# Gate and up blocks of a macaron layer: a second weight sum by accumulating DMA, the lower right tile's product moved to third place, one bank seeded by ScalarE

## The chip, the cores and the metric

The kernel runs on one core of one Trainium2 chip. The metric is the time of one execution on the device, in microseconds; lower is better. Runs of the kernel before: 1727.0, 1727.16 and 1728.76 us, median 1727.16 us.

## What is computed

One decoder layer on a 256 x 2048 float32 input: a half-step SwiGLU FFN, a token mixer with two head groups, a second half-step FFN, a last norm. The change sits in the FFNs:

```python
def swiglu_ffn(x, w_gate, w_up, w_down):
    return (jax.nn.silu(x @ w_gate) * (x @ w_up)) @ w_down

x = x + FFN_RESIDUAL_SCALE * swiglu_ffn(rms_norm(x, ffn1_norm[l]), ...)   # 2048 -> 5632 -> 2048
...
x = x + FFN_RESIDUAL_SCALE * swiglu_ffn(rms_norm(x, ffn2_norm[l]), ...)
return rms_norm(x, final_norm)
```

## The kernel before, in words

**Arithmetic.** Every float32 matrix product is made of three products of rounded parts: both operands are split into a high part (a cast to the float32r type) and a low part (the rest), and hi x hi, lo x hi and hi x lo are added up in PSUM. `parts_of` (L214) splits a weight tile of 128 x 2048 (512 rows of the matrix by 512 columns): two casts of 128 x 1024 on ScalarE make the high part, one subtraction on VectorE makes the low part. Splits go round three pairs of buffers (`split_tiles`, L198), so a cast waits until TensorE has done with the high part made three splits earlier.

**Gate and up blocks.** The 5632 columns of the hidden layer are walked in one first block of 512 columns and five steps s = 0 to 4 of 1024 columns; in each step one block for the gate matrix (`g`) and one for the up matrix (`u`). After s = 0, 2 and 4 a down projection follows (`down`, L793). A gate or up block is one call of `seven` (L417). It handles 2048 rows by 1024 columns of weights: the upper 1024 rows as a 2 x 2 arrangement of tiles w11, w12, w21, w22 by a scheme of seven products in place of eight (two token tiles, two row halves, two column halves), the lower 1024 rows by plain products.

- The seven products, each 12 matmuls of 512 columns (`product_of`, L448): p0 with w11, p4 with w11 + w12, p5 with w11 + w12 + w22, p6 with w12 + w22, p2 with w22, p3 with the sum of p5 plus w21, p1 with w21. The stationary operands (`sf`) are sums of activation tiles made earlier.
- Plain products, each 24 matmuls on two banks (`usual`, L451): b2 and b3 for the right column half, a2 and a3 for the left one.
- Weight sums: w11 += w12, w11 += w22, w11 += w21 on VectorE (L463, L486, L514), in place; w12 += w22 by an accumulating DMA that GpSimd issues (L464).
- PSUM: four banks a, c, e, d. `snap` (L443) copies a bank to SBUF on ScalarE: s1 = a after p0, s5 = c after p4, u2 = -a after p5, u3 = -a after p6. `done(t, n, bank, snapshots)` hands over an output tile: `gate` (L879) or `up` (L884) adds the snapshots to the bank on VectorE (`total`, L871), then SiLU on ScalarE or the product with the gate.
- Order on TensorE: p0, p4, b2, p5, b3, p6, p2, a2, p3, a3, p1. The output tiles are done in the order (1,1) after p6, (0,1) after p2, (1,0) after a3, (0,0) after p1, the last with s1.

**Loads.** All weights come by DMAs on SP's queue, 1 MB each, in the order of `get` (L432): w11, w12, b2, w22, b3, a2, w21, a3. w11 and w12 lie in a pool of two buffers (`kept`), the others in three (`raws`, L81). SP issues in order, and a load waits for its buffer's last reader.

**What sets the order.** The tile framework's planner orders each engine's instructions by data flow and its own estimates; `held` (L41) pins an engine to program order for a while. So a line's place in the program isn't its place on the engine: casts and sums of the next products are moved ahead. Blocks also contain the transposes of finished hidden tiles (`turn_hidden`, L536, called by `settle`).

Of the kernel before, what the change touches and what calls it, by code (L numbers as in the profile page):

```python
# [13 lines left out]
ALU = mybir.AluOpType  # L14
AX = mybir.AxisListType

P = 128
D = 2048
S = 256
FF = 5632  # L20
NT = S // P
# [4 lines left out]
UK = 4  # L26
NH = 8
EPS = 1e-6
SQRT_FLOOR = 2.0**-114


class Engine:
# [17 lines left out]
def hybrid_block(ctx: ExitStack, tc: tile.TileContext, a: dict, out: bass.AP):  # L50
    nc = tc.nc
    Engine.pinned = False
    dve, act, pe, sp = (Engine(tc, e) for e in (nc.vector, nc.scalar, nc.tensor, nc.sync))
# [30 lines left out]

    def bank(name):
        return psum.tile([P, 512], F32, tag="ps", name=name)

    def f32(ap):
        return ap.bitcast(F32)
# [9 lines left out]
    ident = const.tile([P, P], F32, name="ident")  # L99
# [3 lines left out]
    early = const.tile([P, 1], F32, name="early")  # L103
# [110 lines left out]
    def parts_of(raw, name):  # L214
        hi, lo = split_tiles(name)
        for h in (slice(0, 2), slice(2, UK)):
            act.copy(hi[:, h, :], raw[:, h, :])
        low_part(raw, hi, lo)
        return blocks(hi, lo)
# [194 lines left out]
    def quad(tile):  # L414
        return tile.rearrange("p (j c) -> p j c", j=UK)

    def seven(w, rows, cols, sf, xs, name, keep, done, between=None, early=False, own=None, factor=None):  # L417

        apart = {}
        if own:
            a, c = (bank(f"ps_{name}_{n}") for n in "ac")
            apart.update({(t, 1): bank(f"ps_{name}_x{t}1") for t in range(NT)})
            d, e = bank(f"ps_{name}_d"), None
            apart.update({(t, 0): bank(f"ps_{name}_x{t}0") for t in range(NT)})
        else:
            a, c, e, d = (bank(f"ps_{name}_{n}") for n in "aced")  # L430

        def get(u, n, kept=False):  # L432
            src = w[u * UK * P : (u + 1) * UK * P, cols[n] : cols[n] + CW]
            return load(src, f"{name}_{u}{n}", kept=kept)

        (r0, r1), two = rows, len(xs) > 1
        w11, w12 = get(r0, 0, True), get(r0, 1, True)
        b2, w22 = get(xs[0][0], 1), get(r1, 1)
        b3 = get(xs[1][0], 1) if two else None
        a2, w21 = get(xs[0][0], 0), get(r1, 0)  # L440
        a3 = get(xs[1][0], 0) if two else None

        def snap(ps, n, scale=1.0):  # L443
            s = keep(f"{n}_{name}")
            act.activation(s, ps, AF.Copy, scale=factor[n] if factor else scale)
            return s

        def product_of(i, raw, ps, begin=False, end=True, blk=None):  # L448
            multiply([(ps, sf[i], begin, end)], blk or parts_of(raw, f"{name}_p{i}"), True)

        def usual(i, raw, n, *targets, first=None):  # L451

            blk = first or parts_of(raw, f"{name}_x{i}{n}")
            if own:
                last = i == len(xs) - 1
                targets = [(apart[t, n], t, i == 0, last) for t in range(NT)]
            multiply([(ps, stationary(xs[i][1], t), b, z) for ps, t, b, z in targets], blk, True)
            if own and last:
                for t in range(NT):
                    own(t, n, apart[t, n])  # L460

        product_of(0, w11, a, True)
        dve.tensor_tensor(w11, w12, w11, op=ALU.add)  # L463
        nc.gpsimd.dma_start(w12, w22, accum_op=ALU.add)  # L464
        if early:
            between("first sum")
        product_of(4, w11, c, True)
        blk = None
        if early:
            between("second product")  # L470
            hi, lo = split_tiles(f"{name}_x01")
            act.copy(hi, b2)
            s1 = snap(a, "s1")
            dve.tensor_tensor(w11, w22, w11, op=ALU.add)
            low_part(b2, hi, lo)
            blk = blocks(hi, lo)
        else:
            s1 = snap(a, "s1")
        s5 = snap(c, "s5")
        if between:  # L480
            between(0)
        usual(0, b2, 1, (e, 1, True, not two), (c, 0, False, False), first=blk)
        if between:
            between(1)
        if not early:
            dve.tensor_tensor(w11, w22, w11, op=ALU.add)  # L486
        if between:
            between("sum")
        product_of(5, w11, a)
        blk = blk2 = None  # L490
        if early:
            blk = parts_of(b3, f"{name}_x11")
            hi2, lo2 = split_tiles(f"{name}_p2")
            act.copy(hi2, w22)
            blk2 = blocks(hi2, lo2)
        u2 = snap(a, "u2", -1.0)
        if between:
            between(2)
        if two:
            usual(1, b3, 1, (e, 1, False, True), (c, 0, False, False), first=blk)  # L500
        if early:
            between("third sum")
        if early:
            low_part(w22, hi2, lo2)
            between("third low")
        product_of(6, w12, a)
        u3 = snap(a, "u3", -1.0)
        if early:
            between("fifth product")
        done(1, 1, e, [u3, s5])  # L510
        product_of(2, w22, c, blk=blk2)
        done(0, 1, c, [u2])
        usual(0, a2, 0, (d, 0, True, False), (a, 1, False, False))
        dve.tensor_tensor(w11, w21, w11, op=ALU.add)  # L514
        product_of(3, w11, a, end=own is not None or not two)
        if early:
            between("sixth product")
        if two:
            usual(1, a3, 0, (a, 1, False, True), (d, 0, False, False))
        done(1, 0, a, [])  # L520
        product_of(1, w21, d, own is not None)
        done(0, 0, d, [s1])

    def ffn(tag, norm, after, opening=False):
        with tc.tile_pool(name=f"ffn{tag}", bufs=1, side="left") as fp:
            more_from(fp)
            wg, wu, wd = (a[f"ffn{tag}_w_{s}"][0] for s in ("gate", "up", "down"))
# [8 lines left out]
            def turn_hidden(u, t, h, again):  # L536

                if u not in hidden:
                    hidden[u] = big(f"h{tag}_{u}")
                pt = bank(f"ph{tag}_{u}_{t}")  # L540
                for j in range(UK):
                    pe.transpose(pt[:, j * P : (j + 1) * P], h[:, j * P : (j + 1) * P], ident)
                pt = pt.rearrange("p (j c) -> p j c", j=UK)
                hi = hidden[u][:, :, t * P : (t + 1) * P]
                lo = hidden[u][:, :, S + t * P : S + (t + 1) * P]
                act.copy(hi, pt)
                dve.tensor_tensor(lo, pt, f32(hi), op=ALU.subtract)
                if again:
                    act.copy(quad(h), pt)
                    turned[u, t] = quad(h)  # L550

            def settle():
                while waiting:
                    turn_hidden(*waiting.pop(0))
# [3 lines left out]
            units, vs, sf, xn = {}, {}, {}, {}  # L558
# [84 lines left out]
            ps = {(m, t): bank(f"ps_{m}{tag}_0_{t}") for m in "gu" for t in range(NT)}  # L643
# [223 lines left out]
            for s in range(5):  # L867
# [22 lines left out]
                def meanwhile(i):  # L890
# [19 lines left out]
                    elif s == 0 and i == 0:  # L910
                        sums()

                seven(wg, (0, 1), cs, sf, xs, f"g{tag}_{s}", keep, gate, meanwhile, opening and s == 0)
                sp.held = False
                seven(
                    wu, (0, 1), cs, sf, xs, f"u{tag}_{s}", keep, up,
                    (lambda i: settle() if i == 1 else None) if opening and s == 0 else None, 
                )
                if s % 2 == 0:
                    down(s == 4)  # L920
# [49 lines left out]
    with tc.tile_pool(name="mixer", bufs=1, side="left") as mp, tc.tile_pool(name="mixw", bufs=2, side="left") as mw:  # L970
# [171 lines left out]
        def sc_c(between):  # L1142
# [10 lines left out]
            def turn(n):  # L1153
                for f in range(0, 4, 2):
                    pt = bank(f"pt_c{n}_{f}")
                    for i in range(2):
                        for t in range(NT):
                            o = i * S + t * P
                            pe.transpose(pt[:, o : o + P], z[t, n][:, (f + i) * P : (f + i + 1) * P], ident)
                    for i in range(2):  # L1160
                        q = 4 * (1 - n) + f + i
                        c = tmp("cc", q, S + 2, bufs=8)
                        nc.gpsimd.memset(c[:, :2], 0.0)
                        act.copy(c[:, 2:], pt[:, i * S : (i + 1) * S])
                        cc[q] = c

            def done(t, n, ps, tiles):
                for p in tiles[1:]:
                    dve.tensor_tensor(tiles[0], tiles[0], p, op=ALU.add)
                    free.append(p)  # L1170
                if tiles:
                    z[t, n] = tiles[0]
                    dve.scalar_tensor_tensor(z[t, n], ps, rt[t], z[t, n], op0=ALU.mult, op1=ALU.add)
                else:
                    z[t, n] = free.pop()
                    act.activation(z[t, n], ps, AF.Copy, scale=rt[t])
                if (t, n) == (1, 0):
                    turn(1)
# [226 lines left out]
```

## Time and profile before

| | |
|---|---|
| median of 3 runs | 1727.16 us |
| the profiled execution | 1726.91 us |
| its span, first to last instruction | 1725.1 us |
| granted TensorE clock, mean | 0.999 |
| median landing of a 1 MB load of raw_d | 5.2 us |
| HBM read | 339.82 MB |

Each line of the profile names a line of the program, an engine and an operation; the recording helper of the kernel gives nearly all of them line 43, so groups are told apart by their tiles: `hi_u_p` and `lo_u_p` are the parts of an up block's operand of one of the seven products, `hi_u_x` of a plain one, `raw_u` a loaded weight tile, `ps_u_a` the bank a of an up block, `s_u` and `u_u` its snapshots; `g` in place of `u` for gate, `d` for down. A row of the timeline has the start, the time (from the first start to the last end of a merged run, in us), the engine, the operation, output<-input, shapes and the count; in brackets the engine's idle time ahead of it and what ended it. A row of a stretch has its bounds, its length, and for PE, PEld (weight loads), DVE, ACT and POOL the busy time and the count, then the granted clock, the DMA engines' share and GB/s. A row of the view of waits has the waiting instruction, what it waited for, total us, how often, and the longest.

### The profile page before, as it was taken

The page shows a single profiled execution, that of the slowest core. Times are in us where ns is not written, and L with a number is a line of the kernel's source. Part 1 is how long each engine was busy: PE and PEld are TensorE (multiplying, and loading weights), DVE is VectorE, ACT ScalarE, POOL GpSimd, SP SyncE. Part 2 cuts the span into 40 slices and gives each one's busy share as a digit, 9 for nine tenths or more (in the row PEclk, how much of TensorE's full clock was granted, in tenths as well). Part 3 has the DMA queues.
Part 4 walks back from the last instruction along what each step waited for, and adds up shares of the span by engine and source line. Part 5 has one row for each costly group of instructions (what it writes and reads, how often), then busy time and mean ns, then how long its engine had stood idle before and what let it go on. Part 6 is the DMA issues. An engine that isn't in the chain of part 4 may idle for free.

```text
span 1725.1 us, 20426 instructions
## 1 busy us (share of the span) xinstructions
PE 1715.3 (99%) x7985; PEld 1432.9 (83%) x7985; DVE 1452.2 (84%) x1212; ACT 1077.8 (62%) x1406; POOL 35.3 (2%) x62
## 2 busy tenths in 40 slices
PE   9999999999999999999999999999999999999998
PEld 8888888888888888888888888888888888888886
DVE  7988889789789888787897889889788887788886
ACT  7666566656466656666965657655556664556664
POOL 0010000000000000000000000000000000000000
PEclk9999999999999999999999999999999999999999
DMA  8775777667677766655556675776777757677753
GB/s 300 225 258 174 242 234 227 214 236 233 182 238 226 227 201 219 211 160 193 175 197 205 204 251 165 228 237 224 230 227 219 244 171 243 214 225 220 254 179 128
DMA packets 178256, 372.59 MB, mean 216 GB/s; under 512 B 6132, under 2 KB 9072, under 8 KB 174448
## 3 DMA queue, kind: packets, MB, share of 16 engines
q1 hardware_dynamic: 173632, 340.81, 58.4%
q0 software_dynamic: 4352, 29.43, 8.5%
q8 instruction: 62, 1.02, 0.2%
q10 hardware_dynamic: 176, 1.06, 0.2%
q14 instruction: 34, 0.28, 0.0%
HBM read 339.82 MB, written 2.10 MB: 198 GB/s over the span
## 4 chain that ended last, share of the span: by engine, by line
PE 99%; DVE 0%; ACT 0%; DVEq 0%; issue 0%; ACTq 0%
PE ps_d L43 14%; PE ps_in L43 10%; PE ps_g_a L43 9%; PE ps_u_a L43 9%; PE ps_g_c L43 6%; PE ps_u_c L43 6%; PE ps_d_a L43 5%; PE ps_u_d L43 5%; PE ps_g_d L43 5%; PE ps_d_c L43 3%; PE ps_u_e L43 3%; PE ps_g_e L43 3%; PE ps_g L43 3%; PE ps_o L43 3%; PE ps_u L43 3%; PE ps_d_d L43 3%
## 5 line engine op out<-in xcount | busy, mean ns | idle before, releaser
L43 ACT CAST hi_g_p<-raw_g 128x1024 fp32r<-128x1024 f32 (+1 forms) x139 | 142.1, 1054 | 111.6 <-DVE raw_g L43 26.9
L43 DVE TENSOR_TENSOR lo_g_p<-raw_g,hi_g_p 128x2048 fp32r<-128x2048 f32 x70 | 159.8, 2289 | 42.3 <-ACT hi_g_p L43 41.6
L43 DVE TENSOR_TENSOR lo_u_p<-raw_u,hi_u_p 128x2048 fp32r<-128x2048 f32 x70 | 159.3, 2288 | 39.5 <-ACT hi_u_p L43 39.2
L43 ACT CAST hi_u_p<-raw_u 128x1024 fp32r<-128x1024 f32 x140 | 141.3, 1047 | 70.1 <-issue 23.1
L43 PE MATMUL ps_d<-hi_d,h 128*128 128x512 f32 x696 | 166.0, 390 | 0.0
L43 PEld LDWEIGHTS ps_d<-hi_d,h 128*128 128x128 f32 x696 | 130.0, 188 | 26.6
L43 ACT CAST hi_d<-raw_d 128x1024 fp32r<-128x1024 f32 x88 | 88.6, 1048 | 68.3 <-PE ps_u_d L43 19.9
L43 DVE TENSOR_TENSOR lo_d<-raw_d,hi_d 128x2048 fp32r<-128x2048 f32 x44 | 100.8, 2290 | 29.3 <-ACT hi_d L43 29.3
L43 PE MATMUL ps_in<-xT_nm,hi_in 128*128 128x512 f32 x512 | 122.5, 391 | 0.0
L43 ACT CAST hi_d_p<-raw_d 128x1024 fp32r<-128x1024 f32 x84 | 85.2, 1048 | 59.2 <-DVE raw_d L43 33.7
L43 PEld LDWEIGHTS ps_in<-xT_nm,hi_in 128*128 128x128 f32 x512 | 94.0, 188 | 18.8 <-ACT tha L43 0.5
L43 DVE TENSOR_TENSOR lo_d_p<-raw_d,hi_d_p 128x2048 fp32r<-128x2048 f32 x42 | 95.5, 2288 | 15.5 <-ACT hi_d_p L43 15.4
L43 ACT CAST hi_g_x<-raw_g 128x1024 fp32r<-128x1024 f32 (+1 forms) x79 | 81.2, 1058 | 42.9 <-PE ps_g_c L43 25.6
L43 ACT CAST hi_u_x<-raw_u 128x1024 fp32r<-128x1024 f32 x80 | 80.5, 1046 | 36.4 <-PE ps_u_c L43 22.1
L43 DVE TENSOR_TENSOR lo_g_x<-raw_g,hi_g_x 128x2048 fp32r<-128x2048 f32 x40 | 91.5, 2288 | 9.2 <-ACT hi_g_x L43 8.9
L43 DVE TENSOR_TENSOR lo_in<-raw_in,hi_in 128x2048 fp32r<-128x2048 f32 x32 | 73.2, 2288 | 26.7 <-ACT hi_in L43 26.3
L43 DVE TENSOR_TENSOR lo_u_x<-raw_u,hi_u_x 128x2048 fp32r<-128x2048 f32 x40 | 91.4, 2286 | 1.4 <-ACT hi_u_x L43 0.8
L43 PE MATMUL ps_d<-lo_d,h 128*128 128x512 f32 x348 | 86.2, 389 | 0.0
L43 ACT CAST hi_in<-raw_in 128x1024 fp32r<-128x1024 f32 x64 | 64.0, 1045 | 24.9 <-PE ps_in L43 15.2
L43 PEld LDWEIGHTS ps_d<-lo_d,h 128*128 128x128 f32 x348 | 65.3, 188 | 13.6
L43 DVE TENSOR_TENSOR raw_u<-raw_u,raw_u 128x2048 f32<-128x2048 f32 x30 | 68.7, 2289 | 8.5 <-DMA raw_u<-in_ffn_w_up_dram 8.1
L43 DVE TENSOR_TENSOR raw_g<-raw_g,raw_g 128x2048 f32<-128x2048 f32 x30 | 68.7, 2289 | 5.7 <-DMA raw_g<-in_ffn_w_gate_dram 5.2
(477 smaller groups left out, 3750.5 us busy)
## 6 DMA issues: line engine op xcount, KB each, us to landing
raw_d<-in_ffn_w_down_dram SPq DMA_DIRECT2D x88, 1024.0 KB, 5.2
raw_u<-in_ffn_w_up_dram SPq DMA_DIRECT2D x87, 1024.0 KB, 5.3
raw_g<-in_ffn_w_gate_dram SPq DMA_DIRECT2D x86, 1024.0 KB, 5.2
raw_in<-in_w_in_dram SPq DMA_DIRECT2D x32, 1024.0 KB, 5.1
raw_g<-raw_g POOLq DMA_DIRECT2D x10, 1024.0 KB, 7.0
raw_u<-raw_u POOLq DMA_DIRECT2D x10, 1024.0 KB, 7.0
raw_in_c<-in_w_in_dram SPq DMA_DIRECT2D x8, 1024.0 KB, 5.3
raw_o<-in_w_out_dram SPq DMA_DIRECT2D x8, 1024.0 KB, 5.2
```

The source lines that it names most:

```text
L43: ins = getattr(self.engine, name)(*args, **kwargs)
```

## The change

In 16 calls of `seven` (gate and up, s = 1 to 4, both FFNs; `moved=s > 0`) another order is taken. s = 0, the down projections and the mixer stay on the old path.

- **Third weight sum.** p3's operand is finished by a second accumulating DMA, w11 += w21, issued by GpSimd behind p5's split. VectorE's sum is gone. w21 is loaded ahead of a2.
- **p2 third.** The product with w22 follows p4, into bank c on top of it; s5 must be taken out of c in between. The output tile (0,1) is then done after b3, before p6.
- **Seed.** In place of the snapshot s1, ScalarE copies bank a to bank d after p0, and a2 adds onto it without a start flag. The tile (0,0) needs no VectorE add. One block, `g1_3` (`PARTLY`), keeps the snapshot.
- u3 and the split of p3's operand are pinned on ScalarE to program order (`act.held`).
- Transposes in `turn_hidden` and in the mixer's `turn` go through a helper that sets the start flag on the first of four only.

```diff
-        a2, w21 = get(xs[0][0], 0), get(r1, 0)
+        if not moved:
+            a2, w21 = get(xs[0][0], 0), get(r1, 0)
+        else:
+            w21, a2 = get(r1, 0), get(xs[0][0], 0)
...
+        if moved:
+            first = parts_of(w11, f"{name}_p0")
+            dve.tensor_tensor(w11, w12, w11, op=ALU.add)
+            nc.gpsimd.dma_start(w12, w22, accum_op=ALU.add)
+            seeded = name not in PARTLY
+            product_of(0, None, a, True, blk=first)
+            if seeded:
+                act.copy(d, a)
+                s1 = []
+            else:
+                s1 = [snap(a, "s1")]
+            product_of(4, w11, c, True)
+            s5 = [snap(c, "s5")]
+            if between:
+                between(0)
+            product_of(2, w22, c)
+            usual(0, b2, 1, (e, 1, True, not two), (c, 0, False, False))
...
+            dve.tensor_tensor(w11, w22, w11, op=ALU.add)
...
+            product_of(5, w11, a)
+            nc.gpsimd.dma_start(w11, w21, accum_op=ALU.add)
+            u2 = snap(a, "u2", -1.0)
...
+            if two:
+                usual(1, b3, 1, (e, 1, False, True), (c, 0, False, True))
+            done(0, 1, c, [u2])
+            product_of(6, w12, a)
+            act.held = True
+            u3 = snap(a, "u3", -1.0)
+            act.held = False
+            done(1, 1, e, [u3] + s5)
+            usual(0, a2, 0, (d, 0, not seeded, False), (a, 1, False, False))
+            act.held = True
+            fourth = parts_of(w11, f"{name}_p3")
+            act.held = False
+            product_of(3, None, a, end=not two, blk=fourth)
+            if two:
+                usual(1, a3, 0, (a, 1, False, True), (d, 0, False, False))
+            done(1, 0, a, [])
+            product_of(1, w21, d)
+            done(0, 0, d, s1)
+            return
```

The helper for transposes, and one of its two places:

```diff
+    def turn_into(ps, sources):
+        for i, src in enumerate(sources):
+            pe.matmul(
+                ps[:, i * P : (i + 1) * P], src, ident, is_transpose=True, start=i == 0, stop=True,
+                skip_group_check=True,
+            )
...
-                for j in range(UK):
-                    pe.transpose(pt[:, j * P : (j + 1) * P], h[:, j * P : (j + 1) * P], ident)
+                turn_into(pt, [h[:, j * P : (j + 1) * P] for j in range(UK)])
```

More of the change, by code (lines that the diff above doesn't have):

```diff
@@ L29 @@
 SQRT_FLOOR = 2.0**-114
+PARTLY = ("g1_3",)
 class Engine:
@@ L415, in quad, with seven @@
         return tile.rearrange("p (j c) -> p j c", j=UK)
-    def seven(w, rows, cols, sf, xs, name, keep, done, between=None, early=False, own=None, factor=None):
+    def seven(w, rows, cols, sf, xs, name, keep, done, between=None, early=False, own=None, factor=None, moved=False):
         apart = {}
@@ L460, in usual @@
                     own(t, n, apart[t, n])
+        if moved:
[15 more added lines that the diff above has]
+            usual(0, b2, 1, (e, 1, True, not two), (c, 0, False, False))
+            if between:
+                between(1)
+            dve.tensor_tensor(w11, w22, w11, op=ALU.add)
+            if between:
+                between("sum")
+            product_of(5, w11, a)
+            nc.gpsimd.dma_start(w11, w21, accum_op=ALU.add)
+            u2 = snap(a, "u2", -1.0)
+            if between:
+                between(2)
+            if two:
[17 more added lines that the diff above has]
+            return
         product_of(0, w11, a, True)
@@ L911, in meanwhile @@
                         sums()
-                seven(wg, (0, 1), cs, sf, xs, f"g{tag}_{s}", keep, gate, meanwhile, opening and s == 0)
+                seven(
+                    wg, (0, 1), cs, sf, xs, f"g{tag}_{s}", keep, gate, meanwhile, opening and s == 0, moved=s > 0,
+                )
                 sp.held = False
@@ L916, in ffn @@
                     wu, (0, 1), cs, sf, xs, f"u{tag}_{s}", keep, up,
-                    (lambda i: settle() if i == 1 else None) if opening and s == 0 else None,
+                    (lambda i: settle() if i == 1 else None) if opening and s == 0 else None, moved=s > 0,
                 )
@@ L1155, in turn @@
                     pt = bank(f"pt_c{n}_{f}")
[L1156 to L1159, printed above, removed]
+                    turn_into(
+                        pt, [z[t, n][:, (f + i) * P : (f + i + 1) * P] for i in range(2) for t in range(NT)]
+                    )
                     for i in range(2):
```

## The prediction

> **What bounds the kernel now.** I read the page first, then the view of waits for TensorE alone, then busy time by stretches.
>
> ```profile
> span 1725.1 us, 20426 instructions
> PE 1715.3 (99%) x7985; PEld 1432.9 (83%) x7985; DVE 1452.2 (84%) x1212; ACT 1077.8 (62%) x1406; POOL 35.3 (2%) x62
> PEclk9999999999999999999999999999999999999999
> q1 hardware_dynamic: 173632, 340.81, 58.4%
> q0 software_dynamic: 4352, 29.43, 8.5%
> PE 99%; DVE 0%; ACT 0%; DVEq 0%; issue 0%; ACTq 0%
> ```
>
> ```profile
> PE idle L43 <- DVE ones L43: 1.1, 1, 1.1
> PE ps_g L43 <- ACT hi_g L43: 0.6, 1, 0.6
> ```
>
> ```profile
> 241.10:282.90 41.80, 41.80 (x190) 34.66 (x190) 37.19 (x24) 25.49 (x30) 0.85 (x1) 1.00 0.74 230
> 200.30:617.00 416.70, 416.70 (x1868) 345.37 (x1868) 350.23 (x234) 252.19 (x291) 6.89 (x8) 1.00 0.71 225
> 1067.00:1632.00 565.00, 565.00 (x2533) 468.17 (x2532) 476.98 (x300) 340.26 (x393) 9.49 (x11) 1.00 0.71 224
> 1716.90:1725.10 8.20, 0.00 (x1) 0.00 (x0) 2.73 (x10) 1.63 (x4) 0.00 (x0) 0.79 0.48 182
> ```
>
> TensorE is the bound and has no slack. It is busy for 1715.3 of 1725.1 us at the full granted clock; 8.2 us of the rest is the tail behind its last matmul (last row, from 1716.9), 1.7 us the two waits at the start. In the stretch with the first FFN's changed blocks (200.3 to 617) it is busy for 416.70 of 416.70 us, from 1067 to 1632 likewise. VectorE, at 37.19 of 41.80 us in one up block, is loaded but not the bound. The DMA share is 0.71.
>
> "Busy" could hide stretched matmuls, so I look at the rate, in the timeline of that up block (u, s = 1, first FFN). From here T is 241.15 us, its first matmul.
>
> ```profile
> 236.69 2.29 DVE L43 TENSOR_TENSOR raw_u<-raw_u,raw_u 128x2048 f32<-128x2048 f32 x1
> 239.07 2.00 ACT L43 CAST hi_u_p<-raw_u 128x1024 fp32r<-128x1024 f32 x2 [0.74 <-DVE raw_u L43]
> 239.51 0.85 POOL L464 DMA_DIRECT2D raw_u<-raw_u  x1 [42.95 <-DVE raw_u L43]
> 240.97 2.00 ACT L43 CAST hi_u_x<-raw_u 128x1024 fp32r<-128x1024 f32 x2
> 241.10 2.29 DVE L43 TENSOR_TENSOR lo_u_p<-raw_u,hi_u_p 128x2048 fp32r<-128x2048 f32 x1 [2.12 <-ACT hi_u_p L43]
> 241.15 1.98 PE L43 MATMUL ps_u_a<-hi_u_p,x 128*128 128x512 f32 x8
> 245.69 1.07 PE L43 MATMUL ps_u_c<-lo_u_p,xs 128*128 128x512 f32 x4
> 246.11 2.28 DVE L43 TENSOR_TENSOR raw_u<-raw_u,raw_u 128x2048 f32<-128x2048 f32 x1
> 246.59 1.98 PE L43 MATMUL ps_u_e<-hi_u_x,x 128*128 128x512 f32 x8
> 246.88 0.59 ACT L43 ACTIVATE s_u<-ps_u_c 128x512 f32<-128x512 f32 x1
> 248.41 1.98 PE L43 MATMUL ps_u_c<-hi_u_x,x 128*128 128x512 f32 x8
> 253.84 1.07 PE L43 MATMUL ps_u_a<-lo_u_p,xs 128*128 128x512 f32 x4
> 254.04 1.06 ACT L43 CAST hi_u_p<-raw_u 128x1024 fp32r<-128x1024 f32 x1 [1.58 <-PE ps_u_a L43]
> 256.02 2.29 DVE L43 TENSOR_TENSOR raw_u<-raw_u,raw_u 128x2048 f32<-128x2048 f32 x1 [0.88 <-DMA raw_u<-in_ffn_w_up_dram]
> 260.19 1.98 PE L43 MATMUL ps_u_a<-hi_u_p,xs 128*128 128x512 f32 x8
> 262.91 1.98 PE L43 MATMUL ps_u_c<-hi_u_p,xs 128*128 128x512 f32 x8
> 263.21 0.58 ACT L43 ACTIVATE u_u<-ps_u_a 128x512 f32<-128x512 f32 x1
> 265.63 1.98 PE L43 MATMUL ps_u_d<-hi_u_x,x 128*128 128x512 f32 x8
> 267.44 1.98 PE L43 MATMUL ps_u_a<-hi_u_x,x 128*128 128x512 f32 x8
> ```
>
> From 241.15 to 265.63 TensorE issues 108 matmuls of 512 columns: 24.48 us, 0.227 us each, without a wait. So a block costs its matmuls and nothing else: only fewer matmuls, or a higher rate, could make it shorter. VectorE and ScalarE run ahead and wait for buffers that TensorE frees (the cast at 254.04 starts 0.20 us behind the last matmul on an older high part). **That the first up blocks' third sum at 256.02 waited 0.88 us for a load cost nothing.**
>
> **The change, part by part**, for 16 blocks (g and u, s = 1 to 4, both FFNs). p0 to p6 are the seven products, b2, b3, a2, a3 the plain ones.
>
> *TensorE: none removed.* Counting the built program's order: 7076 matmuls of 512 columns, 584 of 256, 301 of 128, in both. p2's 12 matmuls move to stand between the fourth and fifth of b2 (the planner splits b2's first eight). The transposes keep their number and shape. Cost 0. What could be won in these blocks is their idle time, 0.00 us in the rows above.
>
> *VectorE: less.* Out: the third weight sum (2.29 us, row 256.02) in 16 blocks, and in the 15 seeded ones an add that ends the block:
>
> ```profile
> L43 DVE TENSOR_TENSOR s_u<-ps_u_d,s_u 128x512 f32<-128x512 f32 x10 | 6.9, 686 | 0.0
> L43 ACT ACTIVATE ps_u<-ps_u,r_n x4: 653/673/688, 32.5 to 1044.9; 128x512 f32<-128x512 f32 x4
> ```
>
> That is 16 x 2.29 + 15 x 0.69 = 47 us of VectorE work, all beside TensorE's 41 us per block: worth 0 on the path. *ScalarE:* the 0.58 us snapshot becomes a copy from bank to bank. The nearest row, a scaling in place, takes 0.67: +0.1 us per block, hidden while ScalarE has its pauses (25.49 of 41.80 us busy).
>
> *The new order makes one wait tight: the snapshot of bank c.* p4 fills c, ScalarE takes s5 out of it (row 246.88), then TensorE may write c again. Before, eight matmuls on e stand between, so c is due at 248.41 (T+7.26), and s5 ended at 247.47: 0.94 us spare. After, four stand between, so p2 is due on c at T + 28 x 0.227 = T+6.35. When is s5 done? Ahead of it on ScalarE stands, in most blocks, half of p5's cast. This needs p4's high buffer (free at 245.69, +0.20: T+4.74) and the second sum. VectorE now does that sum right behind p4's low part: T-0.05 + 2 x 2.25 = T+4.45, in time. So cast T+4.74 to 5.79, s5 from 5.69 (starts overlap by 0.1, as 239.07 to 240.97 shows for two casts) to 6.28. How fast TensorE resumes is seen once, at the start:
>
> ```profile
> 5.22 0.61 ACT L43 CAST hi_g<-raw_g 128x512 fp32r<-128x512 f32 x1
> 5.89 1.20 PE L43 MATMUL ps_g<-hi_g,xT_n 128*128 128x512 f32 x4 [0.58 <-ACT hi_g L43]
> ```
>
> ScalarE ends at 5.83, TensorE starts at 5.89: 0.06. Its four matmuls then take 1.20, not 3 x 0.227 + 0.39 = 1.07: 0.13 for the restart. So p2 starts near T+6.34, on the due time, and pays up to 0.13 for weights not loaded ahead. I take **0.1 us per block, 16 x 0.1 = 1.6 us**. Bounds: nothing (s5 at its earliest, 0.20 behind p4, ends at 6.23), and one full cast ahead of it, 0.95 x 16 = 15 us. I take the value near the first because the chain, worked from rows, ends there.
>
> *The third sum as an accumulating DMA.* Durations:
>
> ```profile
> raw_u<-raw_u POOLq DMA_DIRECT2D x10, 1024.0 KB, 7.0
> raw_u<-in_ffn_w_up_dram SPq DMA_DIRECT2D x87, 1024.0 KB, 5.3
> DMA to landing us min/median/max: 6.9/7.0/9.1
> ```
>
> The last row is the ten on raw_g. The chain in an up block: low part of p2 follows the second sum, T+6.7; that frees w22's buffer, w21's load goes out on SP and lands at T+12.0; p5's low part (w11's last reader) is done at T+11.2; POOL starts 0.53 after its release (row 236.69 ends at 238.98, POOL 239.51); landing at T+12.0 + 0.53 + 7.0 to 7.5 = T+19.6 to 20.1. p3's casts (2.0 us) cannot start before T+20.0 anyway, when b3's high buffer comes free. Queued behind them on ScalarE: half of a3's cast (it needs p6's high buffer, T+23.8), then the snapshot u3, which can start at T+24.8 and ends at T+25.4. TensorE writes bank a again at T+26.3 (267.44). So p3's casts may end 2.6 us late, landing at T+22.5, before TensorE waits: 2.4 us spare. In the gate blocks of s = 2 and 4 transposes stand ahead of the second sum, p5's low part ends near T+13.8, landing near T+21.3, a SiLU stands in the queue, and the transposes give back 0.8: 0.8 to 1.0 us spare. Cost **0**; if a landing takes 9.1, about 1 us in those four blocks.
>
> *DMA load and SP.* q0's rows: 8.5% of 1725.1 over 29.43 MB is 5.2 us of all 16 engines per accumulate of 1.05 MB; q1: 3.1 us per load. The added 5.2 in a 41.8 us block makes the share 0.74 + 0.12 = 0.86. w21's load now precedes a2's and takes w22's buffer, freed early; the next block's loads are due ten or more us after their issue. A load has shared the engines with an accumulate once, issued at 190.1 with the accumulate at 195.7, and took 7.7 against 5.3:
>
> ```profile
> L43 SPq DMA_DIRECT2D raw_g<-in_ffn_w_gate_dram x1: 368/368/368, 190.1 to 190.1; - x1
> DMA to landing us min/median/max: 7.7/7.7/7.7
> ```
>
> a3's load (out at T+13.5 to 16) will share with the new accumulate, land up to 5.2 late, at T+24 instead of 19 at worst, and is needed at T+23.8: it just fits. Cost 0.
>
> **Sum.** 0 + 0 + 1.6 + 0 = +1.6 us: 1726.91 (the profiled execution, span 1725.1) to 1728.5; on the median of the runs shown, 1727.16, which lies 0.25 above it, 1728.8.
>
> **Rivals.**
>
> *A, slower: s5 is queued too late.* If the second sum ends after T+4.65, or p2's casts slip, each 0.1 us goes straight to TensorE. At half a cast per block, 0.5 x 16 = 8 us: 1735; at the whole, 1742. It decides from 0.1 us of lateness. For it: nothing is spare in that chain. Against: every link is gated by TensorE itself, so lateness doesn't add up.
>
> *B, slower: the accumulate lands late beside loads.* a3's load and the next w11's go out while it runs. If the 16 engines were shared evenly in time, it would take 5.2 + 3.1: landing at T+23.2 in 12 blocks (0.7 late) and T+24.4 in four (about 2 late): 12 x 0.7 + 4 x 2 = 16 us, 1743. It decides from a landing at T+22.5. For it: the share of 0.86. Against: the load slowed at 190.1, while its accumulate took 6.9, like those alone (this block's is one of the ten between 6.9 and 9.1).
> [...]
>
> *C, faster: relieved VectorE shortens blocks.* TensorE would have to be waiting for it now; the rows show 0.00 us. Even with every restart in these blocks gone it is 1 or 2 us: 1726.
>
> **How the numbers follow.** A measurement of this kernel tells about 0.2% (3.5 us) from no change: 1723.7 to 1730.6. The forecast (+0 to 3.4 us) has 0.57; A 0.22; B 0.18; C, if it went beyond 3.5 us by a way that I don't see, 0.03. So same 0.57, slower 0.40, faster 0.03. Predicted 1728.8. Its own range is 1726 to 1730.6; to hold 8 in 10 the range must reach well into A and B, to 1740; below, 1726.
>
> **What would show it.** Waits of TensorE: none, or 16 of 0.1 us at ps_c behind ScalarE's s. Many waits for s of 0.3 us or more would be A. Waits of ps_a for u, or a landing of raw<-raw above 9 us, B. VectorE should lose 47 us of busy time with the span unchanged. A span more than 3 us shorter would show that TensorE's 0.227 us per matmul isn't the floor that I take it for.

## The result, and the profile after

Four runs after: 1735.91 to 1739.37 us, median 1738.86; four before, median 1727.85. The ratio is 1.006 with an interval of 1.0043 to 1.0078: **slower by 0.6%**, 11 us. Five more runs of the same kernel gave a median of 1736.21 against 1728.13, ratio 1.0048 (1.0035 to 1.0060). The time lies in the stated range, but in its slower part: the likeliest case, no change, did not come.

The page of the kernel after (profiled execution 1735.91 us, span 1734.1). The recording helper is line 44 here; the first accumulating DMA of a changed block is line 477, the new one line 497.

```profile
span 1734.1 us, 20440 instructions
...
PE 1721.3 (99%) x7985; PEld 1433.4 (83%) x7985; DVE 1409.4 (81%) x1181; ACT 1077.8 (62%) x1406; POOL 49.2 (3%) x78
...
q1 hardware_dynamic: 173632, 340.81, 57.4%
q0 software_dynamic: 6656, 46.21, 13.9%
...
PE 95%; DMA 2%; DVE 1%; ACT 1%; issue 0%; DVEq 0%; ACTq 0%; POOLq 0%; SPq 0%
```

VectorE has 31 instructions less (16 sums and 15 adds) and TensorE the same 7985, and the span is 9.0 us longer. The chain that ended last is no longer TensorE alone: 2% of it is now DMA. The waits of TensorE after:

```profile
PE ps_u_a L44 <- ACT u_u L44: 2.5, 2, 1.6
PE idle L44 <- DVE ones L44: 1.1, 1, 1.1
PE ps_g_a L44 <- ACT u_g L44: 0.8, 1, 0.8
PE ps_g L44 <- ACT hi_g L44: 0.2, 1, 0.2
```

New are the rows for bank a behind the snapshot u3 (`u_u`, `u_g`). The timeline of the worst block (u, s = 1, second FFN; T = 1261.02):

```profile
1265.79 1.06 ACT L44 CAST hi_u_p<-raw_u 128x1024 fp32r<-128x1024 f32 x1
1266.46 1.07 PE L44 MATMUL ps_u_e<-hi_u_x,x 128*128 128x512 f32 x4
1266.75 0.59 ACT L44 ACTIVATE s_u<-ps_u_c 128x512 f32<-128x512 f32 x1
1267.39 2.11 PE L44 MATMUL ps_u_c<-hi_u_p,xs 128*128 128x512 f32 x8
...
1275.18 0.87 POOL L497 DMA_DIRECT2D raw_u<-raw_u  x1 [14.86 <-DMA raw_u<-in_ffn_w_up_dram]
...
1285.66 1.98 PE L44 MATMUL ps_u_d<-hi_u_x,x 128*128 128x512 f32 x8
1285.74 2.00 ACT L44 CAST hi_u_p<-raw_u 128x1024 fp32r<-128x1024 f32 x2 [5.93 <-DMA raw_u<-raw_u]
1287.64 1.04 ACT L44 CAST hi_u_x<-raw_u 128x1024 fp32r<-128x1024 f32 x1
...
1288.58 0.59 ACT L44 ACTIVATE u_u<-ps_u_a 128x512 f32<-128x512 f32 x1
...
1289.22 2.11 PE L44 MATMUL ps_u_a<-hi_u_x,x 128*128 128x512 f32 x8 [1.59 <-ACT u_u L44]
```

Both suspected waits stand in it. *Bank c:* s5 ends at T+6.32, TensorE goes on at T+6.37, 0.02 us behind its due time, and its eight matmuls take 2.11 instead of 1.98. The view of waits doesn't list this, since the modelled end of the matmul before covers the gap; it is seen in the starts alone. *Bank a:* the accumulate lands 10.46 us after its issue, at T+24.62, and p3's two casts, half of a3's and u3 then run one behind the other on ScalarE (p6's last matmul on bank a ends at T+24.81, u3 starts at T+27.56), until TensorE gets bank a at T+28.20, 1.75 us late.

To add such gaps up, I took the start-to-start times of the matmuls and summed what exceeds 0.227 us: at bank c for p2's matmuls, at bank a for the first eight of a3, which are the ones that wait (where these eight run at half the clock, that counts with it). "Full clock" is when the granted clock rose to 1 at the start:

```
execution           span    bank c  bank a  full clock  half clock later on
before             1725.1     0       0        4.8      -
after              1734.1     2.0     4.3     10.0      -
e0_again           1732.6     2.0     3.6      4.0      -
e8_look            1734.7     2.0     5.1      5.4      3.4 us
e9_look            1740.0     2.0     8.5      9.8      3.4 + 3.4 us
e10_look           1741.4     2.0     7.9      9.6      6.8 + 3.4 us
e1 (sum on VectorE)1728.8     2.0     0        5.6      -
e2 (p2 behind b2)  1728.3     0       1.6      4.7      -
e3 (split late)    1729.4     1.8     0.6      4.5      -
e7 (e2 and e3)     1726.9     0       0.4      5.2      -
```

### The profile page after: what moved, and what is told of

Read it like the earlier page. It is cut to its first block, busy times and chain, and to the rows that moved or that the text cites. A ratio compares the mean times of both kernels' runs of the same rounds, so it can differ in the third digit from the quotient of the medians.

```text
span 1734.1 us, 20440 instructions
## 1 busy us (share of the span) xinstructions
PE 1721.3 (99%) x7985; PEld 1433.4 (83%) x7985; DVE 1409.4 (81%) x1181; ACT 1077.8 (62%) x1406; POOL 49.2 (3%) x78
## 4 chain that ended last, share of the span: by engine, by line
PE 95%; DMA 2%; DVE 1%; ACT 1%; issue 0%; DVEq 0%; ACTq 0%; POOLq 0%; SPq 0%
PE ps_d L44 14%; PE ps_in L44 10%; PE ps_g_a L44 9%; PE ps_u_a L44 9%; PE ps_g_c L44 6%; PE ps_d_a L44 5%; PE ps_u_c L44 5%; PE ps_g_d L44 5%; PE ps_u_d L44 5%; PE ps_d_c L44 3%; PE ps_g_e L44 3%; PE ps_g L44 3%; PE ps_o L44 3%; PE ps_u L44 3%; PE ps_d_d L44 3%; PE ps_u_e L44 2%
## 5 line engine op out<-in xcount | busy, mean ns | idle before, releaser
L44 DVE TENSOR_TENSOR lo_in<-raw_in,hi_in 128x2048 fp32r<-128x2048 f32 x32 | 73.2, 2288 | 27.0 <-ACT hi_in L44 25.6
L44 PEld LDWEIGHTS ps_in<-xT_nm,lo_in 128*128 128x128 f32 x512 | 65.6, 191 | 2.5
L44 PE MATMUL ps_in<-xT_nm,lo_in 128*128 128x256 f32 x512 | 66.4, 283 | 0.0
```

The costliest lines, as they stand in the source:

```text
L44: ins = getattr(self.engine, name)(*args, **kwargs)
```

## The experiments

The theory behind all of them (W): TensorE pays 2 us for the tight snapshot s5 and 4 us or more for late landings of the new accumulate, which reach it through u3's place in ScalarE's queue. Rivals: the new order itself carries the time; the accumulates' load on the DMA engines costs in other ways; the clock belongs to it (K).

**The changed kernel again.** No edit.

> The changed kernel as it stands, a second profile and more runs. The profile after shows 9.0 us more span than before: 2.0 us of TensorE waits at bank c behind the snapshot s5 (27 gaps), 4.3 us at bank a behind the snapshot u3 (8 gaps, in 4 of the 16 blocks), 1.9 us because the full clock of TensorE was granted at 10.0 us in place of 4.8 us, and 0.4 of smaller ones; its other runs took 3 us longer still at a mean granted clock of 0.996 to 0.997 in place of 0.999. Theory W (waits belong to the change, the time of the first clock step does not): the waits at c come back at 2.0 us within 0.3; those at a vary with the landings of the accumulating DMA, 2 to 8 us; the step to the full clock falls anywhere between 4 and 25 us, and the runs of the kernel before show the same spread of the mean clock. Theory K (the waits make the clock dip, so the clock belongs to the change): the granted clock falls below 1 in the middle of the span, behind a wait, and the runs of before beside it all stay at 0.999.

Bank c gave 2.0 again and bank a 3.6, with the start at 4.0: span 1732.6, 1734.37 us. The other four runs took 1735.3 to 1738.62, three of them at a mean clock of 0.997. Of 27 runs of the kernel before on the same chip 26 had 0.999 and one 0.998. So W's sizes hold, but its view of the clock was shaken; see the three further profiles below.

**The third sum back on VectorE.**

```diff
-            nc.gpsimd.dma_start(w11, w21, accum_op=ALU.add)
+            dve.tensor_tensor(w11, w21, w11, op=ALU.add)
```

> Only the third weight sum goes back from the accumulating DMA to VectorE; order, seed and loads stay as changed. Theory W: the waits at bank a behind u3 (4.3 us in the changed kernel) go, the waits at bank c behind s5 (2.0 us) stay; the time is 4 us below the changed kernel at the same clock, 2 to 4 us above the kernel before: 1730 to 1732 us. VectorE gains 16 x 2.29 = 37 us of busy time, beside TensorE. Rival D (the accumulating DMA's load on the 16 engines also delays weights elsewhere): more than 4.3 us is won, and waits for loads vanish too: 1728 to 1729. Rival S (the new order, not the DMA, carries the time): it stays at 1735 or above.

1731.05 us, ratio to before 1.0017 (1.0008 to 1.0026). Its waits of TensorE:

```profile
PE idle L44 <- DVE ones L44: 1.1, 1, 1.1
PE ps_g L44 <- ACT hi_g L44: 0.2, 1, 0.2
```

The waits at bank a are gone, those at c unchanged (2.0). W holds; rival S falls. VectorE does the sums that the change took from it, 1442.9 us busy in place of 1409.4, and the kernel is 5 to 8 us *faster*: relieving VectorE was worth nothing.

**p2 behind all of b2.**

```diff
-            product_of(2, w22, c)
             usual(0, b2, 1, (e, 1, True, not two), (c, 0, False, False))
+            product_of(2, w22, c)
```

> Only p2's place is undone: its product is issued behind the eight matmuls of b2 on bank e in place of between the fourth and the fifth, so that bank c is due about T+7.3 (T: the first matmul of a block) and not T+6.35. Theory W: the 27 gaps at bank c (2.0 us) go to under 0.3 us; the waits at bank a behind the accumulating DMA stay, but change in size, since w22's buffer and so w21's load and the accumulate come about 1 us later: 4 to 9 us. Time within 3 us of the changed kernel: 1734 to 1739. Rival S (the tight snapshot s5 carries the loss, and the rest is clock): 1728 to 1730.

1731.11 us, ratio 1.0019 (1.0010 to 1.0027). The gaps at c are gone. But bank a fell too, to 1.6, against what I expected. In the two worst blocks a3's load now goes out 1.87 and 0.53 us behind the accumulate, where it stood 0.36 us behind and 0.77 us ahead of it in the profile after, and the landings there fell from 10.3 and 10.5 us to 8.3 and 8.6 (why the load's place matters is shown below). So this edit removes more than the one wait that it was meant for. What is left at bank a is mostly the gate block of s = 2, first FFN (1.2 us, landing at T+24.2). Its runs spread from 1727.7 to 1734.68, and the four slowest, from 1732.99 on, have a mean clock of 0.997.

**p3's casts on ScalarE behind u3.** The accumulate stays; only the queue behind it changes.

```diff
-            u3 = snap(a, "u3", -1.0)
+            taken = act.activation(u3, a, AF.Copy, scale=-1.0)
...
+                cast = act.copy(hi[:, h, :], w11[:, h, :])
+                tc.add_manual_dep(cast.ins, taken.ins.name, ..., reason="behind u3")
```

> The accumulating DMA, the order and the seed stay as changed. Only the place of p3's two casts on ScalarE changes: they are held behind the snapshot u3, which in the changed kernel stood behind them in ScalarE's queue, so that a late landing no longer holds u3 up. Theory W: the landings stay as long as before, 7 to 10.5 us from issue, but the waits at bank a (4.3 us) go, since p3's parts are due some 3.5 us after u3's place; the waits at c stay at 2.0 us: 1730 to 1732 us, as without the DMA. If the casts of 2.0 us or the low part behind them then come too late for p3, the waits move to p3's first matmul on bank a, under 1 us each in the four late blocks. Rival D (it is the load on the 16 DMA engines itself that costs): the time stays at 1734 or above.

1731.28 us, ratio 1.0022 (1.0013 to 1.0031). The accumulates still land 8.2 to 11.9 us after issue, and yet bank a costs 0.6 in place of 3.6 to 8.5. The landings of the accumulate (line 497), two waits of TensorE, and the cast of a3's that stands ahead of u3 in the block with the wait at bank a:

```profile
DMA to landing us min/median/max: 8.2/8.4/11.9
PE ps_d_a L44 <- DVE lo_d_p L44: 1.0, 1, 1.0
PE ps_u_a L44 <- ACT u_u L44: 0.3, 1, 0.3
518.79 1.05 ACT L44 CAST hi_u_x<-raw_u 128x1024 fp32r<-128x1024 f32 x1 [5.68 <-DMA raw_u<-in_ffn_w_up_dram]
```

That separates the two: in the block with the landing of 11.9 us, at T+25.35, bank a is on time. The late landing alone costs nothing there; **a late transfer whose consumer has a snapshot behind it on the same engine** does (3.6 to 8.5 us in the changed kernel). Rival D falls as the main cause, but not wholly: the 0.6 us that is left at bank a comes from a3's load, which took 11.0 us beside the accumulate and holds a3's cast ahead of u3. The 1.0 us in the last down projection, behind a low part on VectorE, is a wait that the kernel with the third sum on VectorE has too (0.3 us by the starts), and that the profile after lacks; its cause stays open.

**Both moves.** e2 and e3 in one kernel.

> The changed kernel with both moves of the experiments before it: p2 behind all of b2 (no tight snapshot s5), and p3's two casts on ScalarE behind u3 (a late landing holds nothing up). The accumulating DMA and the seed stay. Theory W: no waits of over 0.3 us in the 16 blocks, mean clock 0.999 in all runs, and the time of the kernel before within 1 us: 1727 to 1729. Rival D (the accumulating DMA costs in another way, through its share of the 16 engines): 2 us or more above the kernel before.

1729.66 us, ratio 1.0007 (0.9998 to 1.0015): the kernel before, within what can be told, with the accumulates and the seed still in. All 11 runs at 0.999.

```profile
PE idle L44 <- DVE ones L44: 1.1, 1, 1.1
PE pt_n L44 <- DMA xres<-in_x_dram: 0.5, 2, 0.4
PE ps_g L44 <- ACT hi_g L44: 0.5, 1, 0.5
```

The view has no wait in the 16 blocks (the starts show 0.4 us at bank a, 0.3 of it again behind a3's load). It isn't faster than before either: there was nothing to win.

**The seed alone.** Old order, three sums on VectorE, the bank copy in place of s1. The helper for transposes stays in as well, here and in all these kernels.

> Only the seed of bank d by ScalarE (15 blocks) is made; order, loads and all three weight sums on VectorE stand as in the kernel before. All theories: no wait of TensorE in the 16 blocks, VectorE 15 x 0.69 = 10 us less busy, and the time that of the kernel before, 1727 to 1729 us, mean clock 0.999. If it is over 1 us slower, the seed's copy on ScalarE has a cost that the argument left out.

1728.86 against 1728.6 us, ratio 1.0004 (0.9995 to 1.0013): worth 0, as predicted, and so is the helper.

**The accumulate alone.** In the old order, against the kernel before (the accumulate stands right behind p5's product, as in the changed kernel, not in the sum's old place):

```diff
-        a2, w21 = get(xs[0][0], 0), get(r1, 0)
+        w21, a2 = get(r1, 0), get(xs[0][0], 0)
...
-            dve.tensor_tensor(w11, w21, w11, op=ALU.add)
+            nc.gpsimd.dma_start(w11, w21, accum_op=ALU.add)
```

> Only the third sum is made by the accumulating DMA, with the load of w21 ahead of a2's; the products stand in the old order (p2 behind p6) and bank d isn't seeded. Theory W: no waits at bank c behind s5, since c is due at T+7.3. The load of w21 needs the first buffer that is freed, b2's in place of w22's, some 3 us later than in the changed kernel, so that the accumulate lands beyond T+22.5 in most blocks; as in the changed kernel, bank a then waits for u3, 0.5 to 3 us in 8 or more blocks: 1735 to 1750 us, clock below 0.999 in the runs with the longest waits. Rival O (the new order is what makes a late landing cost, by u3's place in ScalarE's queue): under 1 us of waits, 1728 to 1730.

1735.47 us, ratio 1.0044 (1.0032 to 1.0056), in W's range but not by W's way: the load of w21 went out at T+4.3 to 7.5, about as in the changed kernel (T+4.3 to 7.3), the mean clock stayed 0.999, and the waits lie elsewhere, the longest in down projections:

```profile
PE ps_d_c L44 <- ACT s_d L44: 2.2, 2, 1.6
PE ps_u_d L44 <- ACT hi_u_x L44: 1.3, 2, 1.0
PE idle L44 <- DVE ones L44: 1.1, 1, 1.1
PE ps_u_a L44 <- ACT u_u L44: 1.0, 4, 0.3
```

In the longest, at 399 us, two small functions, a table load (1.28 us) and a cast stand on ScalarE ahead of the snapshot `s_d`. So this kernel is a third schedule, and its 6.9 us can't be put down to the accumulate alone. This run decides nothing.

**The wait made larger.**

```diff
-            w21, a2 = get(r1, 0), get(xs[0][0], 0)
+            a2, w21 = get(xs[0][0], 0), get(r1, 0)
```

> The changed kernel with one line undone: the load of w21 stands behind a2's again, so w21 takes the next buffer that is freed and its landing, and with it the accumulating DMA, comes 3 to 5 us later. This makes the suspected wait larger on purpose. Theory W: bank a waits for u3 in most of the 16 blocks, 1 to 4 us each, one for one with the landing beyond T+22.5: 1755 to 1785 us. Theory K (long waits of TensorE lower its granted clock): behind some of these waits the profile shows stretches at half the clock in the middle of the span, of 3.4 us or a multiple of it (the steps of the clock seen so far stand at multiples of 3.413 us), a mean clock below 0.997, and matmuls of 0.43 us there; the cost is then more than the sum of the waits. Against K: the clock stays at 1 from the start to the tail.

1818.11 us, ratio 1.0518 (1.0493 to 1.0542), more than W's 1785, at a mean clock of 0.979. The accumulates are issued 2 to 4 us later, 13 of the 16 within 0.6 us of a load's issue (a3's in the gate blocks, the next block's first in the up blocks), and land at T+24.2 to T+29.4. TensorE's waits:

```profile
PE ps_u_a L44 <- ACT u_u L44: 32.4, 8, 5.8
PE ps_g_a L44 <- ACT u_g L44: 30.8, 8, 6.0
```

These 63 us are W's. Of the other 34 us by which its span (1822.0) exceeds that of before, 2.0 are bank c and 1.9 the start; most of the rest is K's (matmuls at half the clock, 23 us by their start-to-start times), and it can be seen: three stretches of the block u, s = 1, first FFN (after the busy times and counts: granted clock, DMA share, GB/s):

```profile
275.00:276.30 1.30, 0.00 (x0) 0.00 (x0) 0.00 (x0) 0.00 (x0) 0.00 (x0) 1.00 0.97 364
276.30:283.10 6.80, 3.18 (x8) 2.50 (x9) 4.61 (x5) 4.37 (x5) 0.00 (x0) 0.50 0.32 102
283.10:300.00 16.90, 16.90 (x80) 14.08 (x79) 14.20 (x11) 9.85 (x12) 0.86 (x1) 1.00 0.76 227
```

Behind a wait of 5.8 us TensorE is granted half its clock for 6.8 us. There are 13 such drops, of 3.4 or 6.8 us, 71.7 us in all.

**The changed kernel three more times.** Does it have such drops too?

> The changed kernel as it stands, one more profile, to see where its runs at a mean granted clock of 0.997 lose 2 to 4 us more than its waits. Theory K, from the kernel with w21 behind a2 (there every stretch of 3.413 us on the clock's grid in which TensorE idled for 1.99 us or more was followed by one at half the clock, and none with up to 1.81 us): a profile with a mean of 0.997 shows one or two stretches of 3.4 us at half the clock behind a wait of bank a of over 2 us, most likely in the second FFN's block u, s = 1, and a span 1.7 to 3.5 us above the sum of its waits; a profile at 0.999 shows none. Rival: the profile with 0.997 has no such stretch, but a later first step to the full clock (beyond 14 us).

> The same kernel and the same question as in the look before it: a stretch of 3.4 or 6.8 us at half the clock behind a wait of over 2 us at bank a if the mean clock of the profiled execution is 0.997, none if it is 0.999.

> The same kernel and the same question as in the two looks before it: a stretch at half the clock behind a wait of over 2 us at bank a if the mean clock is 0.997, none if it is 0.999.

All three came at 0.996 or 0.997 (1736.46, 1741.82 and 1743.22 us), and all three have them: one, two and two, each behind a wait at bank a of 1.9 to 2.7 us, in the blocks u, s = 3, first FFN and u, s = 1, second FFN. The first of e10_look, in stretches and in the timeline of TensorE:

```profile
520.00:525.00 5.00, 2.93 (x13) 2.08 (x12) 0.85 (x1) 2.88 (x4) 0.00 (x0) 1.00 1.02 361
525.00:531.80 6.80, 6.19 (x15) 4.84 (x16) 6.13 (x6) 3.49 (x5) 0.00 (x0) 0.50 0.64 209
531.80:540.00 8.20, 8.20 (x38) 6.76 (x37) 5.93 (x3) 2.00 (x2) 0.00 (x0) 1.00 0.74 253
```

```profile
525.61 3.78 PE L44 MATMUL ps_u_a<-hi_u_x,x 128*128 128x512 f32 x8 [2.68 <-ACT u_u L44]
529.19 1.91 PE L44 MATMUL ps_u_d<-lo_u_x,x 128*128 128x512 f32 x4
...
532.26 2.00 PE L44 MATMUL ps_u_a<-hi_u_p,x 128*128 128x512 f32 x8
```

Eight matmuls take 3.78 us behind the wait and 2.00 seven microseconds later. K holds: to the wait itself comes, by an estimate from these stretches, up to 1.7 us for each 3.4 us at a granted clock of 0.50 (in the kernel with w21 behind a2, 23 us for 71.7). By their mean clock of 0.996 to 0.997 the runs of 1738 us and more that were not profiled probably lose here what the profile after, at 0.999, doesn't show.

What goes with the different landings in these two blocks shows in two executions of one kernel, same block: the accumulate and a3's load, e0_again first. (Rows of the views of line 497 and of `raw_u` on SP: duration of the issue, first and last start; then microseconds from issue to landing.)

```profile
L497 POOL DMA_DIRECT2D raw_u<-raw_u x1: 860/860/860, 508.7 to 508.7; - x1
...
DMA to landing us min/median/max: 8.7/8.7/8.7
```

```profile
L44 SPq DMA_DIRECT2D raw_u<-in_ffn_w_up_dram x1: 368/368/368, 509.3 to 509.3; - x1
...
DMA to landing us min/median/max: 10.8/10.8/10.8
```

And in e10_look:

```profile
L497 POOL DMA_DIRECT2D raw_u<-raw_u x1: 860/860/860, 510.4 to 510.4; - x1
...
DMA to landing us min/median/max: 11.7/11.7/11.7
```

```profile
L44 SPq DMA_DIRECT2D raw_u<-in_ffn_w_up_dram x1: 367/367/367, 510.3 to 510.3; - x1
...
DMA to landing us min/median/max: 6.3/6.3/6.3
```

With the load 0.55 us behind the accumulate, the accumulate goes first and the load takes 10.8; with the load 0.09 us ahead, the load goes first in 6.3 and the accumulate takes 11.7. Over the five profiles of the changed kernel, ten of the 40 up blocks, seven of them from the eleven in which the load is less than 0.5 us behind (load's issue against the accumulate's, the accumulate's first packet after its issue, landing after its issue, all us):

```
load       -0.77  -0.32  -0.09  0.14   0.36   0.40   0.47  0.51  0.55  0.80
1st packet  3.56   4.78   4.95  5.04   3.72   3.25   2.28  1.44  1.42  1.43
landing    10.5   11.4   11.7  11.9   10.3   10.1    9.5   8.6   8.7   9.1
```

In this table the order flips near 0.5 us; with the load 0.5 us or more behind, the first packet came after 1.42 to 1.45 us in every up block, and the landing after 8.4 to 10.2. Holding a3's load back by half a microsecond was not tried, so this part rests on the traces of five executions and not on an edit. It doesn't cover the third late block, g, s = 2 of the first FFN: there the load is 1.83 us behind and the first packet comes after 1.42 to 1.43 us, and still the accumulate lands 9.4 to 9.9 us after its issue in all five profiles, in place of the 8.3 of the other gate blocks of s = 2 and 4. Why stays open.

## Why the prediction was right and wrong

- *TensorE none, VectorE less, worth 0; seed 0:* right. 31 VectorE instructions fewer (42.8 us of busy time; the 47 counted ends that overlap the next start), the same matmuls, and the kernels with the seed alone and with both moves end at the time of before.
- *s5 on bank c, 1.6 us:* right in mechanism and nearly in size. Due T+6.35, TensorE there at T+6.37, 0.13 for the restart; 2.0 us in all, gone when p2 stands behind b2. Rival A (0.5 us a block) did not come.
- **The step that failed is "The third sum as an accumulating DMA ... Cost 0".** The deciding point was nearly right: in up blocks of the profile after a landing at T+23.8 cost 1.0 us and one at T+24.6 1.75, so it lies at T+22.8 to 22.9 (22.5 in the text). The landing was wrong. I took 7.0 to 7.5 us from accumulates that ran with almost no load beside them (not one load in all, as the text has it: in the profile before five overlap an accumulate by 1 to 2.5 us, none for its whole time); the new one runs beside three or four and took 8.1 to 11.9 in the changed kernel. With w21's own load of 5.1 to 6.8 us, up blocks landed at T+20.9 to 25.6 in place of T+19.6 to 20.1, gate blocks of s = 2, 4 at T+22.5 to 24.2 in place of 21.3. My caveat used 9.1 as the worst case, since that was the longest row of before. The other "just fits", a3's load at T+24 at worst, was short too: it landed at up to T+25.2 beside the accumulate, and what this cost, 0.3 to 0.5 us, shows in the kernels in which u3 no longer waits for the accumulate.
- *Rival B* was the right place and sign (its marks, a wait of ps_a for u and landings above 9 us, are there), with a wrong picture: not even sharing at 0.7 to 2 us in all 16 blocks, 16 us, but three late blocks, in two of them by who is first, 3.6 to 8.5 us with the half-clock matmuls at bank a. That 11 us lies between the forecast and B's 16 is no merit of B's sum: its blocks and terms were others.
- A slip without weight: the matmuls of 128 columns are 314 in both traces, with 11 smaller ones (301 in the text).
- The price of a wait was taken as its length. The clock made it more (eight matmuls in 3.78 us in place of 2.00 behind a wait of 2.68): this and a later first rise to the full clock (at 9.6 to 10.1 us in four of the six profiles of this kernel and the one with w21 behind a2, at 4.0 to 5.6 in all others) make up most of the rest of the 11 us. Why the start differs stays open; it is worth 1.9 us (the block g, s = 0 of the first FFN begins at 55.07 us in the profile after and at 53.19 before).
- *The reason against B* was one load that took 7.7 us beside an accumulate of 6.9, a single case. The runs agree with it only so far that loads creep while an accumulate runs (8 to 11 us in place of 5.2); once both run, the packets of the profile alternate about one to one (below). And a load that is first kept the accumulate's first packet off until 2.3 to 5.0 us after its issue in place of 1.4; that I left out.

## What to carry to other kernels

Take a transfer's duration from rows with the neighbours that it will have, and write down what stands behind its consumer on the same engine: here 2.5 us of lateness were harmless once a snapshot stood ahead of the casts. Work taken from an engine that wasn't the bound (42.8 us of VectorE's) was worth nothing here, and the resource that took it over cost; ask for its slack in microseconds per block, not for its busy share. On this kernel, which keeps TensorE full, waits of 1.9 to 2.7 us had a second price in the granted clock in three of five profiles of the changed kernel (0.50 for 3.4 or 6.8 us), so compare the mean clock of every run and not only the one that was profiled.

## What the runs showed of the hardware

*In these profiles the clock dropped after idle times of about 2 us.* Changes of the granted clock stand on a grid of 3.413 us (from its first rise the full clock lasted 1716.904 us in the profile before and 1720.317 in the profile after: 503 and 504 steps). In the profiles here, ahead of the tail, a step of that grid at the full clock in which TensorE idled for 1.98 us or more was followed by one or two at half the clock in all 17 cases, likewise one with 1.88; one with 1.95 and all with 1.81 or less were not. So the idle time that sufficed here is about 1.9 us in a step.

*Accumulates and loads alternated packet by packet once both ran.* For 5 us of the accumulate in e0_again, and for 3 us of e10_look in which it waited (queue: packets, MB, share of 16 engines):

```profile
q0 software_dynamic: 112, 0.92, 94.0%
q1 hardware_dynamic: 129, 0.25, 14.7%
```

```profile
q1 hardware_dynamic: 399, 0.82, 84.1%
```

112 packets of 8 KB against 129 of 2 KB: about one to one. By their starts they come in rounds of about 0.7 us, 16 of the accumulate and 17 of the loads in each. So the loads get 0.05 MB per us in place of 0.27, and loads out at that time take 8 to 11 us in place of 5.2. In the other stretch the accumulate, already issued, has no packet at all.
